# A planned order for the projection of an attention layer, with half of the values moved behind the queries

## The chip, the core and the metric

The kernel runs on one core of one Trainium2 chip. Its time is the device time of one execution in microseconds; a kernel is given by the median of its runs. The engines are TensorE (PE; PEld is its load of the stationary operand), VectorE (DVE), ScalarE (ACT), GpSimd (POOL) and SyncE (SP), which issues the DMA transfers. Each engine works through its own instructions in order and waits on semaphores for the others. TensorE writes to PSUM, which here is cut into eight banks of 128 x 512 float32 values.

## The reference

A two-layer encoder works on 1024 tokens of width 1024. Only the first mixer, grouped-query attention, is touched by the change:

```
h   = rmsnorm(x, attn_norm)
qkv = h @ w_qkv                   # 16 query heads, 4 key heads, 4 value heads of 64
q   = rope(rmsnorm(q, q_gain)) * 64 ** -0.5
k   = rope(rmsnorm(k, k_gain))    # row and column rotation over a grid of width 64
p   = softmax(q @ k.T)            # 1024 x 1024 for each query head
x   = x + concat(p @ v) @ w_o
```

Behind it come, in both layers, a cross attention into 256 memory tokens and a gated MLP with a convolution, and in the second layer a pooling mixer. All of that stays as it is.

## The kernel before, in words

**Numbers in two parts.** A float32 product is made of three TensorE products on a rounded high part and a low remainder (`mm3`, L738 to L743: high x high, high x low, low x high). A split is a copy on ScalarE (L668) and a subtraction on VectorE (L669).

**Tiles of the projection.** `attention` (L757) works on eight tiles of 128 tokens. The row tile is loaded (`load`), its root mean square is taken on ScalarE and GpSimd (`row_rstd`, L719), the row is scaled on VectorE (L727), turned on TensorE (L735) and split into the slots `hT`. A piece of the weights is 1024 x 256, loaded in two halves of 512 KB into row buffers `scr` (six in all) and split into a pair of slots (`stage_piece`, L679). There are a piece for the keys, one for the values and one for each of four groups of query heads, which is staged twice, once for each half of the tokens. One product of a tile with a piece has 24 TensorE instructions (`piece_gemm`).

**Heads.** Each key or query tile of 128 x 256 then goes through a chain: square on ScalarE (L835), sum on VectorE (L836), root on GpSimd (`rstd`, L714 and L716), scaling (L842), two crossed multiplies (L849) and a straight one (L851) with the tables on VectorE, an add on GpSimd (L852), a split on ScalarE and VectorE (keys L857 and L858, queries L668 and L669 on `qst`), a turn on TensorE (keys L865, queries L878), and copies out of PSUM (L868, L879). The tables of cosine and sine are made on GpSimd from `rope` and the two gains (`tables`, L798 to L819).

**The order of the steps.** The loop `step(i)` (L942) runs over 40 items: eight items of a key and a value tile, then 32 query tiles (half, group, tile). Step i splits item i - 3 and rotates item i - 2, stages a quarter of the next weight piece, prepares row i + 2, does the products of item i and turns item i - 4. The lag is thus fixed, and each engine gets its instructions in the order in which the steps name them. Behind the last three items the scores of the first three units are added (`early`, L788, called at L960).

**Behind the projection.** `units` are 128 pairs of a query block and a head. `scores` (L766) makes a 128 x 1024 score in the bank pair pA (L776), its maximum (L780), the exponential with its sum (L783), the inverse (L785) and the scaling on GpSimd (L786). `turn_p` turns and splits the probabilities, `values` (L996) multiplies them with the values (L1007, L1008). During the projection there is one pA and six banks pB, during the attention two and four.

**The planner.** Class `Plan` (L157) is used by the later stages of the kernel. An operation is added with a kind (engine, least time, time per element, delay, L163), keys that it reads and writes, and places in pools that it takes. `run` gives TensorE's operations their order as they were added; a due time for each of the others follows backwards from those that need them, and a list scheduler with these estimated costs then issues the operations of all engines, at most 30 us ahead of their due time.

Of the kernel before, what the change touches and what calls it, by code (L numbers as in the profile page):

```python
# [40 lines left out]
TA, E0, ES, EN = 0, 3, 2, 3  # L41
# [583 lines left out]
class Kernel:  # L625
# [131 lines left out]
    def attention(self):  # L757
# [8 lines left out]
        def scores(u):  # L766
            if u in prs:
                return
# [5 lines left out]
            for kh in range(2):  # L774
                for part in range(2):
                    nc.tensor.matmul(s[:, kh * 512:(kh + 1) * 512], q,  # L776
                                     R.v(K[part][kh], 4)[:, kv],
                                     start=part == 0, stop=part == 1)
            nm = self.stat(1, "nm")
# [8 lines left out]
        def early(u):  # L788
            if u < EN:
                scores(u)  # L790

        with tc.tile_pool(name="qk", bufs=1, reuse_waits="tile") as qk, self.psum("psq", 1, 6) as self.ps:
            T = [qk.tile([P, 2048], F32R, name=f"T{i}") for i in range(2)]
            wk, wv, w0 = [T[0], T[1]], [R.get(), R.get()], [R.get(), R.get()]
            gain = None
            tabs = {}

            def tables():  # L798

                tab = qk.tile([P, NT, 2, HD], F32, name="tab")  # L800
                nc.sync.dma_start(out=tab.rearrange("p t i c -> p t (i c)"),
                                  in_=a["rope"].rearrange("(t p) c -> p t c", p=P))
                gq = self.cst.tile([P, HD], F32, name="gq")
                gk = self.cst.tile([P, HD], F32, name="gk")
                for g, row in ((gq, a["attn_q_gain"][0]), (gk, a["attn_k_gain"][0])):
                    nc.sync.dma_start(out=g, in_=bass.AP(tensor=row.tensor, offset=row.offset, ap=[[0, P], [1, HD]]))
                nc.gpsimd.tensor_scalar(gq, gq, HD ** -0.5, 1.0, op0=OP.mult, op1=OP.mult)
                tk = self.scr().rearrange("p (t i c) -> p t i c", t=NT, i=2)
                for dst, g in ((tk, gk), (tab, gq)):
                    nc.gpsimd.tensor_tensor(out=dst[:, :, 0], in0=tab[:, :, 0],  # L810
                                            in1=g[:, None, :].to_broadcast([P, NT, HD]), op=OP.mult)
                    d6, t6 = (x[:, :, 1].rearrange("p t (x i c) -> p t x i c", x=2, i=2) for x in (dst, tab))
                    g4 = g.rearrange("p (x i c) -> p x i c", x=2, i=2)
                    for x in range(2):
                        for i in range(2):
                            nc.gpsimd.tensor_tensor(out=d6[:, :, x, i], in0=t6[:, :, x, i],
                                                    in1=g4[:, None, x, 1 - i].to_broadcast([P, NT, ROPE_PAIRS]),
                                                    op=OP.mult)
                tabs["k"], tabs["q"] = tk, tab  # L819

            hT = [[R.get() for _ in range(4)] for _ in range(2)]

            def lhs(t):
                return lambda k: self.blk(hT[t // 4], k, slice((t % 4) * P, (t % 4 + 1) * P))

            def piece_gemm(p, t, ws):
                wh, wl = (self.R_(s).rearrange("p (a b) -> p a b", a=8) for s in ws)
                for k in range(NK):
                    ah, al = lhs(t)(k)
                    self.mm3(p, ah, al, wh[:, k], wl[:, k], k == 0, k == NK - 1)  # L830

            def head_rstd(p):
                ss = self.stat(4, "ss4")
                sq = qk.tile([P, 256], F32, name="sq", bufs=2)
                nc.scalar.activation(sq, p, AF.Square)  # L835
                nc.vector.tensor_reduce(ss, sq.rearrange("p (h c) -> p h c", h=4), axis=AX.X, op=OP.add)  # L836
                return self.rstd(ss, 4, HD)

            def roped(p, r, tab, t):
                qn = qk.tile([P, 256], F32, name="qn", bufs=2)  # L840
                q3 = qn.rearrange("p (h c) -> p h c", h=4)
                nc.vector.tensor_tensor(out=q3, in0=p.rearrange("p (h c) -> p h c", h=4),  # L842
                                        in1=r[:, :, None].to_broadcast([P, 4, HD]), op=OP.mult)
                b = qk.tile([P, 256], F32, name="rb", bufs=2)
                q5 = qn.rearrange("p (h x i c) -> p h x i c", h=4, x=2, i=2)
                b5 = b.rearrange("p (h x i c) -> p h x i c", h=4, x=2, i=2)
                s5 = tab[:, t, 1].rearrange("p (x i c) -> p x i c", x=2, i=2)
# [13 lines left out]
            def turn_k(kst, t):  # L861
                for i in range(2):
                    p = self.psB().rearrange("p (a b) -> p a b", a=4)
                    for h in range(4):
                        nc.tensor.transpose(p[:, h, :], kst[:, h, i:i + 2].rearrange("p a b -> p (a b)").bitcast(F32),  # L865
                                            self.ident)
# [1033 lines left out]
```

## Time and profile before

| what | us |
| --- | --- |
| median of 3 runs | 2549.89 |
| lowest and highest run | 2549.88 and 2550.58 |
| the profiled execution, its own time | 2550.72 |
| its span in the profile | 2548.9 |
| TensorE busy | 2497.3 (98%) |
| VectorE busy | 1992.3 (78%) |
| ScalarE busy | 1344.8 (53%) |
| GpSimd busy | 386.7 (15%) |

The span runs from the first to the last instruction in the trace; the time of the execution has some overhead around it. A row of a timeline gives start, duration, engine, line and operation with its tiles; a bracket at its end gives the idle time of the engine before it and what ended it. A row of the table of stretches gives busy time and number of instructions for each engine, then the granted TensorE clock, the share of time that the DMA engines were busy, and the GB/s that they moved. A row of the waits gives the waiting instruction, what it waited for, the sum in us, how often, and the longest. A row of the groups gives how often an instruction came, its busy time, the mean duration in ns and the idle time before it. TensorE counts as busy while any matmul is in flight, and a matmul's duration overlaps that of the next, so the pace is read from start to start.

### The profile page before, as it was taken

The numbers are of one execution on the slowest core, as the hardware profiler recorded it, in microseconds if no ns is written. First come the engines' busy times: TensorE is split into PE (matmuls) and PEld (weight loads), VectorE is DVE, ScalarE is ACT, GpSimd is POOL, SyncE is SP. The second block draws the span as 40 slices with busy tenths as digits, with TensorE's granted clock in tenths as the row PEclk, the third lists the DMA queues.
The fourth block names the chain that finished last, engine by engine and source line by source line (L and its number), as shares of the span: only waits on it lengthen the run. The fifth ranks groups of instructions, "written<-read, shape, count | busy, mean of one in ns | idle before, by whom it ended". The sixth has DMA issues, their size and how long they took to land.

```text
span 2548.9 us, 37005 instructions
## 1 busy us (share of the span) xinstructions
PE 2497.3 (98%) x13481; PEld 2135.8 (84%) x13481; DVE 1992.3 (78%) x2937; ACT 1344.8 (53%) x2286; POOL 386.7 (15%) x533
## 2 busy tenths in 40 slices
PE   7999999999999999999999999999999999999998
PEld 7998888888889888888887888889888888887886
DVE  5778999993886479888878776887559888887775
ACT  4547888872545346554455433655436545545441
POOL 3564555540002000000000002102000000000001
PEclk9999999999999999999999999999999999999999
DMA  4200000032486123433447663388223324337651
GB/s 151 83 18 1 1 1 1 1 122 86 141 299 230 64 67 111 124 103 88 120 149 257 209 195 104 115 281 282 78 74 108 112 85 122 104 110 265 232 186 66
DMA packets 296203, 315.20 MB, mean 124 GB/s; under 512 B 12501, under 2 KB 235069, under 8 KB 296021
## 3 DMA queue, kind: packets, MB, share of 16 engines
q1 hardware_dynamic: 296021, 312.84, 37.6%
q8 instruction: 106, 1.74, 0.3%
q14 instruction: 76, 0.62, 0.1%
HBM read 227.23 MB, written 80.74 MB: 121 GB/s over the span
## 4 chain that ended last, share of the span: by engine, by line
PE 80%; DVE 9%; issue 3%; ACT 3%; POOL 2%; DMA 2%; SPq 0%; DVEq 0%; ACTq 0%; POOLq 0%
PE pB L741 21%; PE pB L743 21%; PE pB L742 21%; PE pA L743 3%; PE pA L741 3%; PE pA L742 3%; DVE nm L780 2%; PE pB L735 2%; PE pA L776 2%; PE pB L1007 1%; POOL qn L852 1%; DVE R L663 1%; DVE PT L669 1%; PE pB L1008 1%; ACT scr L783 1%
## 5 line engine op out<-in xcount | busy, mean ns | idle before, releaser
L741 PE MATMUL pB<-R,R 128*128 128x512 f32 (+1 forms) x2750 | 1023.4, 372 | 7.9 <-DVE scr L435 1.6
L742 PE MATMUL pB<-R,R 128*128 128x512 f32 (+1 forms) x2750 | 1016.2, 370 | 0.2 <-DVE R L669 0.2
L743 PE MATMUL pB<-R,R 128*128 128x512 f32 (+1 forms) x2730 | 1008.8, 370 | 3.6 <-DVE R L663 3.5
L741 PEld LDWEIGHTS pB<-R,R 128*128 128x128 f32 x2750 | 518.1, 188 | 102.2 <-DVE R L663 3.4
L743 PEld LDWEIGHTS pB<-R,R 128*128 128x128 f32 x2730 | 514.3, 188 | 92.1 <-DVE R L663 5.3
L742 PEld LDWEIGHTS pB<-R,R 128*128 128x128 f32 x2750 | 518.3, 188 | 86.4 <-DVE R L669 0.7
L660 ACT ACTIVATE R<-scr 128x512 fp32r<-128x512 f32 (+2 forms) x318 | 237.0, 780 | 238.8 <-DMA scr<-Gs 59.6
L663 DVE TENSOR_TENSOR R<-X,R 128x512 fp32r<-128x512 f32 x374 | 252.1, 685 | 65.7 <-ACT R L660 64.9
L660 ACT ACTIVATE R<-X 128x512 fp32r<-128x512 f32 x374 | 231.7, 630 | 133.8 <-PE pB L742 65.5
L663 DVE TENSOR_TENSOR R<-scr,R 128x512 fp32r<-128x512 f32 (+2 forms) x318 | 271.0, 882 | 23.8 <-ACT R L660 23.8
L714 POOL TENSOR_SCALAR ms<-ss 128x1 f32<-128x1 f32 (+2 forms) x102 | 24.4, 239 | 1715.3 <-ACT R L722 661.5
L433 ACT COPY scr<-pB 128x512 f32<-128x512 f32 x156 | 91.2, 586 | 196.9 <-PE pB L743 191.0
L786 POOL TENSOR_SCALAR scr<-scr,inv 128x1024 f32<-128x1024 f32 x128 | 144.5, 1129 | 165.8 <-DVE inv L785 160.9
L783 ACT ACTIVATE scr<-pA,nm 128x1024 f32<-128x1024 f32 x128 | 143.1, 1118 | 44.5 <-DVE nm L780 41.9
L669 DVE TENSOR_TENSOR PT<-pB,PT 128x512 fp32r<-128x512 f32 x256 | 163.7, 680 | 2.8 <-ACT PT L668 1.8
L1570 DVE TENSOR_TENSOR X<-pB,X 128x512 f32<-128x512 f32 x144 | 99.2, 690 | 78.9 <-PE pB L743 76.3
L780 DVE TENSOR_REDUCE nm<-pA 128x1 f32<-128x1024 f32 x128 | 156.0, 1219 | 0.5 <-PE pB L735 0.3
L735 PE MATMUL pB<-ident,scr 128*128 128x128 f32 x1088 | 144.6, 276 | 9.1 <-DVE scr L727 7.9
L741 PE MATMUL pA<-R,R 128*128 128x512 f32 (+1 forms) x416 | 149.5, 359 | 2.5 <-ACT R L660 2.5
L735 PEld LDWEIGHTS pB<-ident,scr 128*128 128x128 f32 x1088 | 124.2, 142 | 32.7 <-POOL scr L786 14.9
L743 PE MATMUL pA<-R,R 128*128 128x512 f32 (+1 forms) x416 | 148.9, 358 | 0.5 <-DVE R L663 0.5
L742 PE MATMUL pA<-R,R 128*128 128x512 f32 (+1 forms) x416 | 148.6, 357 | 0.5 <-DVE R L663 0.5
(145 smaller groups left out, 3535.9 us busy)
## 6 DMA issues: line engine op xcount, KB each, us to landing
X<-in_ffn_w_up SPq DMA_DIRECT2D x82, 512.0 KB
Gs<-X SPq DMA_DIRECT2D x100, 256.0 KB
scr<-in_ffn_w_down SPq DMA_DIRECT2D x44, 512.0 KB
scr<-Gs SPq DMA_DIRECT2D x56, 384.0 KB
scr<-Wt SPq DMA_DIRECT2D x40, 512.0 KB
scr<-in_xattn_w_kv SPq DMA_DIRECT2D x32, 512.0 KB
scr<-Gs SPq DMA_DIRECT2D x28, 512.0 KB
scr<-in_attn_w_qkv SPq DMA_DIRECT2D x20, 512.0 KB
```

What stands on the lines that cost most here:

```text
L433: self.nc.scalar.copy(out, p)
L660: self.nc.scalar.activation(hi, src, AF.Copy)
L663: self.nc.vector.tensor_tensor(out=lo, in0=src, in1=hi.bitcast(F32), op=OP.subtract)
L669: nc.vector.tensor_tensor(out=lo, in0=src, in1=hi.bitcast(F32), op=OP.subtract)
L735: self.nc.tensor.transpose(p[:, k, :], src[:, b * P:(b + 1) * P], self.ident)
L741: mm(out, ah, bh, start=start, stop=False)
L742: mm(out, ah, bl, start=False, stop=False)
L743: mm(out, al, bh, start=False, stop=stop)
L780: nc.vector.tensor_reduce(nm, s, axis=AX.X, op=OP.max, negate=True)
L783: nc.scalar.activation(pr, s, AF.Exp, bias=nm, accum_out=rs)
L786: nc.gpsimd.tensor_scalar(pr, pr, ri, 1.0, op0=OP.mult, op1=OP.mult)
L1570: nc.vector.tensor_tensor(out=x, in0=banks[b], in1=x, op=OP.add)
```

## The change

The loop of steps and its helpers are replaced by a plan. What is computed for each tile is the same; the order of the instructions on every engine is now found by `Plan.run`. TensorE's own order is given by a new list, and the turn of an item stands `LAG` = 4 products behind its product:

```diff
-TA, E0, ES, EN = 0, 3, 2, 3
+QKV = (("K", 0), ("V", 0), ("K", 1), ("V", 1), ("K", 2), ("V", 2), ("K", 3), ("V", 3),
+       ("K", 4), (0, 0, 0), (0, 0, 1), ("K", 5), (0, 0, 2), (0, 0, 3), ("K", 6), (0, 1, 0), (0, 1, 1), ("K", 7), (0, 1, 2), (0, 1, 3),
+       *((h, g, t) for h in range(2) for g in range(4) if h or g > 1 for t in range(4 * h, 4 * h + 4)),
+       ("V", 4), ("S", 0), ("V", 5), ("S", 1), ("V", 6), ("S", 2), ("V", 7))
+LAG = 4
```

Keys and values alternate only for the first four tiles. Keys 4 to 7 stand between the first eight queries (half, group, tile), and the values of tiles 4 to 7 stand behind all queries, each followed by one of the three early scores. Since the value weights have been overwritten by then, they are staged a second time (`late`):

```diff
+                    if kind == "V":
+                        if t == 0:
+                            plan_weights("V", (NH + NKV) * HD, 1)
+                        elif t == 4:
+                            plan_weights("late", (NH + NKV) * HD, 0)
```

Every operation becomes an entry with its kind, its size and its keys. The head of a key or query tile:

```diff
+                plan.add("copy", 350, square, [b], [sq], [("sq", sq)], [b])
+                plan.add("add", 340, reduce, [sq], [ss], uses=[sq])
+                plan.add("scale", 2.9, rstd, [ss], [ss])
+                plan.add("add", 340, scaled, [b, ss], [qn], [("qn", qn)], [b])
+                plan.add("add", 490, crossed, [qn, tabkey], [rb], [("rb", rb)], [qn, *used])
+                plan.add("add", 360, straight, [qn, tabkey], [qn], uses=[qn, *used])
+                plan.add("scale", 2.4, both, [qn, rb], [qn], uses=[qn, rb])
```

A product with its places, the split of a value tile, and the early scores:

```diff
+                plan.add("product", 12.4, emit, [("hT", t, g) for g in range(2)] + [("w", s, g) for g in range(2)], [b],
+                         [("B", b)], gives=gives)
...
+                plan.add("copy", 360, lambda: self.high(v[:, :, :HD], src()), [b], [("V", t)], uses=[b])
+                plan.add("add", 340, lambda: self.low(v[:, :, :HD], v[:, :, HD:], src()), [b, ("V", t)], [("V", t)], uses=[b])
...
+                plan.add("tap", 1024, biggest, [s], [("nm", u)], uses=[s])
+                plan.add("square", 1024, exp, [s, ("nm", u)], [x], [("scr", None)], [s], late=4.0)
+                plan.add("tiny", 1, inverse, [x], [("inv", u)], late=6.0)
+                plan.add("scale", 2.7, scale, [("inv", u), x], [x], late=7.0)
```

The tables are no longer made in one go: load, scaling, cosine and sine of both tables are entries of their own (`plan_tables`), as are load, square, norm, turn and split of a row (`plan_rows`) and load and split of each weight half (`plan_weights`). The pools are declared as six `scr`, one pA, six pB, two each of `sq`, `qn` and `rb`, three `qst` and the free slots.

Two things follow for the instruction streams. TensorE's number of instructions stays the same. VectorE and ScalarE get two instructions more and SP two loads more, for the second staging of the value weights. From the fourth score on (the start of the attention) all five engines have the same instructions in the same order as before.

More of the change, by code (lines that the diff above doesn't have):

```diff
@@ new lines, in plan_turn_k, with turn, put @@
+            def plan_turn_k(t):
+                half = ("kst", t)
+                for i in range(2):
+                    b = ("kturned", t, i)
+                    def turn(i=i, b=b):
+                        kst = R.hv(at[half])[:, :768].rearrange("p (h i c) -> p h i c", h=4, i=3)
+                        p = at[b] = self.psB().rearrange("p (a b) -> p a b", a=4)
+                        for h in range(4):
+                            nc.tensor.transpose(p[:, h, :], kst[:, h, i:i + 2].rearrange("p a b -> p (a b)").bitcast(F32),
+                                                self.ident)
+                    def put(i=i, b=b):
+                        o = R.v(K[i][t // 4], 4)[:, :, (t % 4) * P:(t % 4 + 1) * P]
+                        (nc.vector.tensor_copy if i else nc.scalar.copy)(o, at.pop(b))
+                    plan.add("turn", 4, turn, [half], [b], [("B", b)], [half])
+                    plan.add("add" if i else "copy", 512, put, [b], [("KT", t, i)], uses=[b])
```

398 lines of the change are left out of this document (228 added, 170 removed).

## The prediction

> **What bounds the kernel now.** I read the stretches of 20 us first, then TensorE's waits before 206 us (the first weighted sum of values starts at 206.38), then the timeline of each engine where these pointed. Behind that point the two kernels issue the same instructions in the same order on all five queues; only buffer and DMA queue numbers differ. So the whole difference is made in the first 206 us, and all that follows moves with it.
>
> ```profile
> core 0: us, PE busy (x) PEld busy (x) DVE busy (x) ACT busy (x) POOL busy (x), PEclk, DMA share, GB/s
> 20.00:40.00 20.00, 17.24 (x124) 17.04 (x123) 8.42 (x16) 6.22 (x13) 10.50 (x19) 0.83 0.25 85
> 180.00:200.00 20.00, 13.76 (x81) 11.02 (x80) 14.59 (x34) 8.94 (x20) 11.50 (x16) 0.74 0.00 1
> ```
> ```profile
> PE pB L735 <- DVE scr L727: 7.9, 1, 7.9
> PE pB L878 <- DVE qst L669: 6.5, 6, 2.6
> PE pB L743 <- DVE R L669: 3.9, 3, 2.8
> ```
>
> TensorE is the bound, with three holes: the start (7.9 us until the first row is normalised), the stretch from 20 to 40 us, and the one around 180 to 200 us. In the last two the granted clock falls as well, to 0.83 and 0.74.
>
> The pace between the holes is that of the query tiles: 24 products and a turn of four transposes.
>
> ```profile
> 120.76 0.60 PE L878 MATMUL pB<-ident,qst 128*128 128x128 f32 x4
> 121.11 0.36 PE L741 MATMUL pB<-T,R 128*128 128x256 f32 x1
> 124.00 0.60 PE L878 MATMUL pB<-ident,qst 128*128 128x128 f32 x4
> ```
>
> A turn takes 0.35 us from start to start, the 24 products 2.89, together 3.24; four queries need 12.96.
>
> The chain of the head (square, sum, root, scale, rotate, add, split) is slower. In the chain of waits GpSimd's add comes back at
>
> ```profile
> 112.14 1.60 POOL qn L852
> 126.30 1.59 POOL qn L852
> ```
>
> that is every 14.16 us for four queries (the two other long ones between belong to the same four). So from query to query TensorE uses up its lag of four steps; by the end the chain is late:
>
> ```profile
> 186.04 1.09 PE L776 MATMUL pA<-R,R 128*128 128x512 f32 x4
> 187.29 0.63 PE L878 MATMUL pB<-ident,qst 128*128 128x128 f32 x4 [0.15 <-DVE qst L669]
> 190.23 1.12 PE L878 MATMUL pB<-ident,qst 128*128 128x128 f32 x4 [2.31 <-DVE qst L669]
> 193.97 1.09 PE L878 MATMUL pB<-ident,qst 128*128 128x128 f32 x4 [2.63 <-DVE qst L669]
> 199.32 1.11 PE L878 MATMUL pB<-ident,qst 128*128 128x128 f32 x4 [0.38 <-DVE qst L669]
> 203.79 1.03 PE L735 MATMUL pB<-ident,scr 128*128 128x128 f32 x8
> 204.58 1.17 PE L776 MATMUL pA<-R,R 128*128 128x512 f32 x4
> 206.38 0.36 PE L1007 MATMUL pB<-PT,R 128*128 128x256 f32 x1
> ```
>
> The last product ends at 186.04 (the second score starts there); the last query is turned 13.28 us later, and between them TensorE has nothing but turns and scores.
>
> **The change, part by part.**
>
> *The tail.* From 186.04 to 206.38 are 20.34 us. At full pace this holds five query turns (0.35 each), scores 1 and 2 (0.94 each, bounded from 187.29 - 186.04 = 1.25 with its wait and taken from the 0.9 to 1.0 that a score takes at 204.58), and then three turns of probabilities (203.79 to 204.58: 0.79) with scores 3 and 4 between them: 1.75 + 1.88 + 2.37 + 1.88 = 7.9. The hole is 12.4 us. The change takes four products of values, 4 x 2.89 = 11.6 us, out of the front and lays them here, with the three scores between them. TensorE's order is now: turn, V4, turn, S0, V5, turn, S1, V6, turn, S2, V7, turn, then the attention. Counted from the end of the last query's product, at full pace: V4 ends at 3.2, S0 at 4.5, V5 at 7.4, S1 at 8.7, V6 at 11.6, S2 at 12.9, V7 at 15.8, the last turn at 16.1, and with the 4.25 of probabilities and scores values could start at 20.4.
>
> What is late next? There is one score buffer (pA), so S1 waits for the exponential of S0:
>
> ```profile
> L780 DVE TENSOR_REDUCE nm<-pA 128x1 f32<-128x1024 f32 x4 | 4.9, 1214 | 0.0
> L783 ACT ACTIVATE scr<-pA,nm 128x1024 f32<-128x1024 f32 x4 | 4.5, 1119 | 3.0 <-DVE nm L780 3.0
> L668 ACT ACTIVATE R<-pB 128x512 fp32r<-128x512 f32 (+1 forms) x24 | 11.8, 525 | 25.5 <-PE pB L743 19.3 <-PE pB L735 6.2
> L879 ACT CAST R<-pB 128x512 fp32r<-128x512 f32 x32 | 18.6, 580 | 0.2 <-PE pB L878 0.2
> ```
>
> S0 ends at 4.5, its maximum (1.21) at 5.8, its exponential (1.12 and the read of the sum) at 7.1: before 7.8, when S1 is due. VectorE stands at the maximum of S0 from about 1 to 4.5 with the split of query 37 behind it; that split is done at 6.1 and its turn due at 7.4. The next two splits, behind the maximum of S1, end by 10.4 and 12.2 and are due at 11.6 and 15.8. So no turn waits. But in ScalarE's order the copies of V5, V6 and V7 and of the last three queries stand behind the exponential of S2, which ends at 15.5: three at about 0.4 (half rows; bounded by 0.52, the mean of the mixed group) and three at 0.58, some 2.7 us, to 18.2. The split of the first probabilities is behind them. From there copy, subtraction, maximum and the second subtraction bring the first values to 22.3 instead of 20.4. On equal work the kernel before needs 20.34 + 11.6 + 0.94 (S0 was issued earlier) = 32.9; the new one 22.3. **Gain 10.6.** Bounds: 12.5 if the copies cost nothing, 8 if the six banks make the last turns wait for them once more (2.7).
>
> *The front.*
>
> ```profile
> 17.81 1.28 DVE L727 SCALAR_TENSOR_TENSOR scr<-scr,rs 128x1024 f32<-128x1024 f32 x1 [0.72 <-POOL rs L716]
> 23.11 1.03 PE L735 MATMUL pB<-ident,scr 128*128 128x128 f32 x8
> 26.84 0.28 PE L741 MATMUL pB<-T,R 128*128 128x256 f32 x1
> 30.00 0.58 PE L743 MATMUL pB<-T,R 128*128 128x256 f32 x1 [2.76 <-DVE R L669]
> 34.87 0.41 PE L735 MATMUL pB<-ident,scr 128*128 128x128 f32 x1
> 28.06 1.28 DVE L727 SCALAR_TENSOR_TENSOR scr<-scr,rs 128x1024 f32<-128x1024 f32 x1 [5.88 <-POOL rs L716]
> 29.27 1.61 DVE L669 TENSOR_TENSOR R<-pB,R 128x512 fp32r<-128x512 f32 x3
> 24.01 1.74 POOL L816 TENSOR_TENSOR tab<-tab,gq 128x128 f32<-128x128 f32 x4
> ```
>
> The third key tile's products take 34.87 - 26.84 = 8.03 us instead of 2.89. The low half of its rows (29.27) stands on VectorE behind the norm of the next row (28.06), and this behind eleven table instructions in one run on GpSimd, the last at 24.01, and a head's root. The plan sets the roots between the table instructions, and the low half ahead of the next norm. Followed through: GpSimd now takes the first key table before the root of row 2, so that norm moves from 17.8 to about 21.7, just before its turn at 23.1; the key tables end near 25.5, the low half near 27.5, and the products wait 0.6 instead of 2.76, with less of the slow clock (0.58 for a 0.28 product). **Gain 4.5**, between 0 (the root stays late) and 5.1.
>
> *Smaller waits* of TensorE come from the old order of steps too:
>
> ```profile
> 46.65 0.38 PE L743 MATMUL pB<-T,R 128*128 128x256 f32 x1 [0.51 <-DVE R L669]
> 62.67 0.38 PE L741 MATMUL pB<-T,R 128*128 128x256 f32 x1 [0.98 <-DVE R L669]
> ```
>
> These are 1.5, and once the lag is used up each four queries take 14.16 instead of 12.96; for the last two groups before 186 us that is 2.4 more (an estimate from the two paces). Of 3.9 I take **3**, between 0 and 4.5 (with restarts).
>
> *The middle.* Keys 4 to 7 now run beside eight queries. VectorE's rows:
>
> ```profile
> L836 DVE TENSOR_REDUCE ss<-sq 128x4 f32<-128x256 f32 x40 | 16.6, 414 | 4.3 <-ACT sq L835 4.3
> L842 DVE TENSOR_TENSOR qn<-pB,rs 128x256 f32<-128x256 f32 x40 | 16.7, 417 | 0.4 <-POOL rs L716 0.4
> L849 DVE TENSOR_TENSOR rb<-qn,tab 128x128 f32<-128x128 f32 x64 | 15.8, 287 | 1.0
> L669 DVE TENSOR_TENSOR T<-scr,T 128x1024 fp32r<-128x1024 f32 x10 | 12.2, 1220 | 1.5 <-ACT T L668 1.5
> ```
>
> A head costs 0.41 + 0.42 + 2 x 0.29, and about 0.42 each for its second multiply and its split: 2.25, twelve heads 27; two norms 2.6, six low halves of rows 3.9, six key copies 4.1, five or six weight halves 6 to 7. That is 44 us, some 41 when overlapping issue is taken off, against TensorE's 43 (twelve products, three row turns, five key and five query turns). Level, but with a lag of four products ahead of each turn I cost it at nothing; if the cover is gone it costs up to 4.
>
> *Added:* the value weights are fetched and split a second time: two loads of 512 KB on SP (the DMA is idle there), two copies on ScalarE, two subtractions of 1.22 on VectorE. Each lies in the query stretch, where TensorE needs 12.96 per four queries. I put four queries of the new VectorE order in line by hand (head steps of neighbouring queries interleaved instead of one after the other): 12.2 with both weight halves. So the chain no longer loses time on TensorE: 0, at worst 14.16 - 12.96 = 1.2 for each of the six last groups, 7.
>
> [...]
>
> ```profile
> 165.64 0.74 POOL L852 TENSOR_TENSOR qn<-qn,rb 128x256 f32<-128x256 f32 x1 [1.00 <-DVE qn L851]
> 195.51 0.73 POOL L852 TENSOR_TENSOR qn<-qn,rb 128x256 f32<-128x256 f32 x1 [1.23 <-ACT R L879]
> 195.56 0.95 DVE L851 TENSOR_TENSOR qn<-qn,tab 128x256 f32<-128x256 f32 x1
> ```
>
> GpSimd's add takes 0.74 by itself and 1.6 beside a weight subtraction; VectorE's multiply takes 0.95 instead of 0.42 when the add started first. The new order puts rotations of the next query beside this add. My 12.2 already lets each rotation wait for the add. [...]
>
> **The sum.** 10.6 + 4.5 + 3 = 18.1 us. The profiled execution took 2550.72 (span 2548.9), the median is 2549.89; the difference of 0.8 is small against the terms, and I take the sum off the median: **2532**.
>
> **The rivals.**
> [...]
> 2. *The plan doesn't do what it says*: its costs are estimates, and a turn placed behind a late copy opens new waits, so that the tail's 10.6 is given back. For: the one score buffer, and six banks all held at the last turn. Against: the due times above. Gain about 0 to 5: 2547.
> 3. *Slower*: a weight half that lands late. The loads share the row buffers: four are free beside gain and key table. ScalarE's copy of a half stands ahead of the squares, so a load that must wait for the turn of the next row (a row comes every 11 us: key, two queries and turns) stops all heads for up to 11 us, 8 of them beyond one query step. Three such halves cost 24 against the gain of 18, +6: 2556. It decides when more than two of the eight halves in the middle wait so. Against: in the order in which buffers come free, SP waits for the turn of the row before, not of the next.
>
> **Chances.** Forecast 0.62 (2527 to 2537), rival 1 0.21, rival 2 0.09, rival 3 0.08. The bounds of the terms (12.5 + 5.1 + 4.5 = 22, and 8 + 0 + 0) give 2528 and 2542; range 2526 to 2543. A measurement can tell 0.2%, 5 us, from no change: faster 0.87, same 0.06, slower 0.07.
>
> **What would show it.** Right: no wait on `qst` over 0.5 us before the attention; TensorE busy and granted 1.00 in the 20 us before the first values, which start near 188; the third key tile's products under 4 us. [...]

## The result, and the profile after

The changed kernel takes 2533.73 us (median of 4 runs, 2531.66 to 2536.19) against 2550.23 us for the kernel before on the same chips: a ratio of 0.993, 95% interval 0.9913 to 0.9948. Timed again later it took 2533.46 us (5 runs) against 2550.47, ratio 0.9933 (0.9921 to 0.9945). That is 16.5 to 17 us less; 2532 was forecast. The profiled execution took 2532.28 us with a span of 2530.5.

The stretches of the changed kernel, to be set beside those of the prediction (columns: length, busy time and count of TensorE, its weight loads, VectorE, ScalarE and GpSimd, granted clock, DMA share, GB/s):

```profile
20.00:40.00 20.00, 18.26 (x154) 17.86 (x153) 14.26 (x26) 10.71 (x23) 16.64 (x27) 1.00 0.24 80
40.00:60.00 20.00, 20.00 (x174) 20.00 (x173) 17.52 (x35) 11.94 (x23) 11.64 (x16) 1.00 0.34 107
160.00:180.00 20.00, 20.00 (x163) 19.58 (x162) 16.11 (x38) 8.27 (x18) 13.13 (x16) 1.00 0.00 1
180.00:200.00 20.00, 18.86 (x139) 17.22 (x139) 16.38 (x27) 15.78 (x31) 6.90 (x7) 1.00 0.00 1
```

Where TensorE had 17.24 at a clock of 0.83 and 13.76 at 0.74, it now has 18.26 and 18.86 at 1.00, and from 40 to 180 us each stretch is full. All that TensorE waited for before 190 us (engine, tile and line, releaser: us in total, times, longest):

```profile
PE pB L856 <- DVE scr L851: 7.9, 1, 7.9
PE pB L747 <- DVE R L667: 1.7, 2, 1.1
PE pB L745 <- ACT R L664: 1.2, 1, 1.2
PE pB L739 <- ACT R L1020: 1.1, 1, 1.1
PE pB L988 <- DVE R L973: 0.7, 1, 0.7
```

The waits for a query's split (`qst`, 6.5 us before) are gone. What is left is the start (7.9) and single waits of 0.6 to 1.2 us. The tail, in TensorE's timeline (start, duration, line, tiles; in brackets the idle time before and its releaser):

```profile
167.36 0.60 PE L1014 MATMUL pB<-ident,qst 128*128 128x128 f32 x4
170.96 1.17 PE L778 MATMUL pA<-R,R 128*128 128x512 f32 x4
175.13 1.17 PE L778 MATMUL pA<-R,R 128*128 128x512 f32 x4
179.30 1.17 PE L778 MATMUL pA<-R,R 128*128 128x512 f32 x4
183.11 0.60 PE L1014 MATMUL pB<-ident,qst 128*128 128x128 f32 x4
185.29 0.66 PE L739 MATMUL pB<-ident,scr 128*128 128x128 f32 x4 [1.14 <-ACT R L1020]
189.29 0.37 PE L1133 MATMUL pB<-PT,R 128*128 128x256 f32 x1
```

The last query's products end at 167.36, the three scores lie 4.17 us apart with a product of values between each two, the last query is turned at 183.11, and the first weighted sum of values ("first values" from here on) starts at 189.29 instead of 206.38. So 17.1 of the 18.4 us between the spans are made before this point.

The third key tile:

```profile
28.17 0.28 PE L745 MATMUL pB<-T,R 128*128 128x256 f32 x1
29.65 0.39 PE L747 MATMUL pB<-T,R 128*128 128x256 f32 x1 [1.08 <-DVE R L667]
32.33 0.93 PE L856 MATMUL pB<-ident,scr 128*128 128x128 f32 x7
```

Its products take 32.33 - 28.17 = 4.16 us, against 8.03. That is just over the 4 us that the prediction named as a sign.

### The profile page after: what moved, and what is told of

It reads as the page before. It is cut to its first block, busy times and chain, and to the rows that moved or that the text cites. A ratio compares the mean times of both kernels' runs of the same rounds, so it can differ in the third digit from the quotient of the medians.

```text
span 2530.5 us, 37018 instructions
## 1 busy us (share of the span) xinstructions
PE 2488.5 (98%) x13481; PEld 2132.1 (84%) x13481; DVE 2000.4 (79%) x2939; ACT 1347.1 (53%) x2288; POOL 397.5 (16%) x533
## 4 chain that ended last, share of the span: by engine, by line
PE 85%; DVE 7%; issue 2%; ACT 2%; DMA 2%; POOL 1%; DVEq 0%; SPq 0%; ACTq 0%; POOLq 0%
PE pB L745 22%; PE pB L747 22%; PE pB L746 22%; PE pA L747 3%; PE pA L745 3%; PE pA L746 3%; PE pA L778 2%; DVE nm L788 2%; PE pB L739 2%; PE pB L1133 1%; DVE R L667 1%; DVE PT L673 1%; PE pB L1134 1%; ACT scr L791 1%; PE pB L323 1%
## 5 line engine op out<-in xcount | busy, mean ns | idle before, releaser
L664 ACT ACTIVATE R<-scr 128x512 fp32r<-128x512 f32 (+2 forms) x330 | 250.2, 791 | 240.6 <-PE pB L746 56.2
L718 POOL TENSOR_SCALAR ms<-ss 128x1 f32<-128x1 f32 (+2 forms) x102 | 34.3, 336 | 1694.5 <-ACT R L726 661.3
L667 DVE TENSOR_TENSOR R<-scr,R 128x512 fp32r<-128x512 f32 (+2 forms) x330 | 285.1, 893 | 18.8 <-ACT R L664 18.3
L778 PE MATMUL pA<-R,R 128*128 128x512 f32 x512 | 145.1, 405 | 0.0
L672 ACT ACTIVATE PT<-pB 128x512 fp32r<-128x512 f32 x256 | 138.8, 596 | 11.1 <-PE pB L739 10.2
```

Source lines behind the costliest of these rows:

```text
L664: self.nc.scalar.activation(hi, src, AF.Copy)
L667: self.nc.vector.tensor_tensor(out=lo, in0=src, in1=hi.bitcast(F32), op=OP.subtract)
L672: nc.scalar.activation(hi, src, AF.Copy)
L778: nc.tensor.matmul(s[:, kh * 512:(kh + 1) * 512], q, R.v(K[part][kh], 4)[:, kv], start=part == 0, stop=part == 1)
```

## The experiments

The prediction's largest term says that the tail is empty and the moved values fill it. The rival reading, formed after the first result, is that the tail is long because the heads come late, and that their order alone would shorten it. As everything before the attention shows in the time of the first values, I give that time for each run beside the whole. "Behind" is the profiled span less the first values. Both come from one profiled execution for each run; the changed kernel's two profiles have their first values 0.6 us apart, so steps of that size in this column say little.

Each ratio is to the kernel before on the same chip, where it took 2551.31 us (experiments 1 to 4), 2550.47 (the changed kernel again, 5 to 7), 2551.54 (8 to 10) and 2550.63 (11). The changed kernel was run a second time beside some of the others:

> The changed kernel once more, unchanged, so that the others of this call can be set against it: 2532 to 2536, first values at 188 to 190 us.

| kernel | median us (runs) | ratio to before on the same chip, 95% | first values | behind |
|---|---|---|---|---|
| before | 2550.23 (4) | 1 | 206.38 | 2342.5 |
| changed | 2533.73 (4) | 0.993 (0.9913 to 0.9948) | 189.29 | 2341.2 |
| changed, again | 2533.46 (5) | 0.9933 (0.9921 to 0.9945) | 188.71 | 2344.8 |
| 1 values in front | 2548.67 (11) | 0.999 (0.9981 to 0.9999) | 200.78 | 2347.2 |
| 2 before, stages exchanged | 2544.0 (6) | 0.997 (0.9959 to 0.9982) | 197.06 | 2345.7 |
| 3 before, values behind | 2549.78 (11) | 0.9994 (0.9985 to 1.0003) | 200.63 | 2346.8 |
| 4 before, query tables later | 2548.37 (11) | 0.9988 (0.9979 to 0.9997) | 202.24 | 2343.2 |
| 5 before, all three | 2540.22 (5) | 0.9958 (0.9945 to 0.997) | 192.43 | 2345.3 |
| 6 tables in one run | 2537.74 (5) | 0.9946 (0.9934 to 0.9959) | 190.50 | 2345.4 |
| 7 staged twice | 2538.25 (5) | 0.9952 (0.9939 to 0.9966) | 190.69 | 2345.4 |
| 8 scores last | 2546.51 (11) | 0.9981 (0.9972 to 0.999) | 202.18 | 2343.9 |
| 9 copies early | 2536.61 (5) | 0.9945 (0.9933 to 0.9958) | 190.36 | 2343.3 |
| 10 scores early | 2534.31 (5) | 0.9934 (0.992 to 0.9947) | 188.35 | 2345.6 |
| 11 three more | 2535.67 (5) | 0.994 (0.9926 to 0.9954) | 189.43 | 2343.3 |

### 1. The plan without the moved values

```diff
-       ("K", 4), (0, 0, 0), (0, 0, 1), ("K", 5), (0, 0, 2), (0, 0, 3), ("K", 6), (0, 1, 0), (0, 1, 1), ("K", 7), (0, 1, 2), (0, 1, 3),
-       *((h, g, t) for h in range(2) for g in range(4) if h or g > 1 for t in range(4 * h, 4 * h + 4)),
-       ("V", 4), ("S", 0), ("V", 5), ("S", 1), ("V", 6), ("S", 2), ("V", 7))
+       ("K", 4), ("V", 4), ("K", 5), ("V", 5), ("K", 6), ("V", 6), ("K", 7), ("V", 7),
+       *((h, g, t) for h in range(2) for g in range(4) for t in range(4 * h, 4 * h + 4)))
...
-                        elif t == 4:
-                            plan_weights("late", (NH + NKV) * HD, 0)
...
-                for _, f in todo:
+                for n, (_, f) in enumerate(todo):
                     if f:
                         f()
+                    if n < 3:
+                        plan_scores(n)
```

> The changed kernel with the values of tiles 4 to 7 back among the keys; nothing is staged twice, and the three early scores stand between the last turns. The plan stays. Theory F (what the prediction's largest term says: behind the last query TensorE has a hole of 12.4 us, and only moved products fill it): it loses about 10.6 us against the changed kernel, 2543 to 2545, with some 20 us from the end of the last product to the first values. Theory C (the hole is mostly the late chain of the heads, and the plan brings the chain on time whatever the tail holds): last turn some 7 us behind the last product instead of 13.3, scores then 3.5 us apart for the one score buffer, first values 12 to 14 us behind the last product; it loses only 2 to 5 us, 2535 to 2539.

TensorE's timeline of this kernel, from the end of the last query's product (178.70):

```profile
178.70 0.60 PE L1013 MATMUL pB<-ident,qst 128*128 128x128 f32 x4
180.52 0.66 PE L1013 MATMUL pB<-ident,qst 128*128 128x128 f32 x4 [1.22 <-DVE qst L666]
180.93 1.17 PE L777 MATMUL pA<-R,R 128*128 128x512 f32 x4
184.18 0.63 PE L1013 MATMUL pB<-ident,qst 128*128 128x128 f32 x4 [2.07 <-DVE qst L666]
188.48 0.73 PE L777 MATMUL pA<-R,R 128*128 128x512 f32 x2 [1.78 <-ACT scr L1042]
192.32 1.09 PE L738 MATMUL pB<-ident,scr 128*128 128x128 f32 x8 [2.21 <-ACT scr L1042]
200.78 0.37 PE L1132 MATMUL pB<-PT,R 128*128 128x256 f32 x1
```

The tail takes 22.1 us: turns wait for splits, the third score and the first turn of probabilities wait for exponentials. First values come 11.5 us later than in the changed kernel. Theory F said 10.6, theory C at most 5. With the plan, then, it is the moved values that shorten the tail. (Its tail without them is also 6.3 us longer than that of the next experiment, which holds one score less.) The whole time is 4 to 6 us above what F gave; most of that lies behind the first values and is taken up at the end.

### 2. The old steps with two stages exchanged

```diff
-                for lag, stage in ((3, split), (2, rope)):
+                for lag, stage in ((2, rope), (3, split)):
```

> The kernel before, with the two stages of a step exchanged: a head is rotated before the split of the head before it, so VectorE's low half no longer waits for GpSimd's add and ScalarE's copy ahead of the next rotation. Nothing else. Theory F: the chain's pace falls from 14.16 to about 12.2 us per four queries, TensorE's waits for the query's split of 2.4 us go, and the tail keeps its hole: gain 2 to 3, 2547 to 2548. Theory C: the turns of the tail come on time too (2.31 and 2.63 and most of the 13.28 us to the last turn): gain 7 to 10, 2540 to 2543. If the order of the two stages is not what sets the chain's pace: 2550.

TensorE's timeline:

```profile
181.31 1.09 PE L776 MATMUL pA<-R,R 128*128 128x512 f32 x4
186.88 1.92 PE L776 MATMUL pA<-R,R 128*128 128x512 f32 x4 [2.44 <-ACT scr L783]
190.45 1.11 PE L878 MATMUL pB<-ident,qst 128*128 128x128 f32 x4 [0.79 <-DVE qst L669]
197.06 0.37 PE L1007 MATMUL pB<-PT,R 128*128 128x256 f32 x1
```

What VectorE waited for in the kernel before, from 60 to 180 us, in the first row of that view:

```profile
DVE qst L669 <- ACT qst L668: 21.4, 26, 1.0
```

One exchanged pair brings the first values forward by 9.3 us, and here theory C is right: the last product ends at 181.31 instead of 186.04 (4.7 us), and the tail behind it takes 15.75 us instead of 20.34 (4.6). In the old order VectorE's low half of a head stood ahead of the next rotation and waited for GpSimd's add and ScalarE's copy, 21.4 us in all; behind the rotation it waits for neither, and this row is gone from the same view. The hole of 12.4 us thus had two causes: late heads (4.6) and, as the next experiment and the fifth show, too little work beside the scores (the rest). The whole time, 2544.0, is 1 us above theory C's range.

### 3. The old steps with the values behind

```diff
-                if i < NT:
-                    piece_gemm(p[:, :256], i, wk)
-                    turn_h(i + 1)
-                    piece_gemm(p[:, 256:], i, wv)
+                if i < NT or i >= len(items):
+                    if i < NT:
+                        piece_gemm(p[:, :256], i, wk)
+                        turn_h(i + 1)
+                        if i >= 4:
+                            rs[i] = head_rstd(p[:, :256])
+                            return
+                        piece_gemm(p[:, 256:], i, wv)
+                    else:
+                        ps.pop(i)
+                        i -= len(items) - 4
+                        piece_gemm(p[:, 256:], i, wv)
...
+                if n == len(order):
+                    return self.stage_piece(w, (NH + NKV) * HD, wv)
...
-                if 0 <= i < len(items):
+                if 0 <= i < len(items) + 4:
```

> The kernel before, steps and lag as they were, with the values of tiles 4 to 7 computed in the four steps behind the last query and their weights staged a second time. Theory F: the hole is filled without any plan: gain 8 to 11, 2539 to 2542. Theory C: the four products cover the late chain, so the gain is of the same size here, 7 to 10, but it is not to be had a second time beside the exchanged stages. Rival (the fixed steps can't use it: copies of the values and the late splits stand in each other's way, or keys 4 to 7 without a second product run into VectorE): gain under 4, over 2546.

TensorE's timeline, beside the fifth key tile and at the end:

```profile
49.19 0.38 PE L741 MATMUL pB<-T,R 128*128 128x256 f32 x1 [0.62 <-ACT R L868]
51.29 0.39 PE L743 MATMUL pB<-T,R 128*128 128x256 f32 x1 [1.60 <-DVE R L669]
200.63 0.37 PE L1021 MATMUL pB<-PT,R 128*128 128x256 f32 x1
```

The last query's product ends at 177.3 (the fourth of the last group in the timeline). From there to the first values are 23.3 us; with the first score, which is issued ahead here, 24.3 on the work of the prediction's 32.9: 8.6 gained in the tail, within the 8 to 11 of theory F. But 5.75 is all that arrives. Keys 4 to 7 now follow each other with one product of 2.9 us each, and these wait for the low halves of the rows and for ScalarE's copies; TensorE is busy 16.24 of the 20 us from 40 to 60, where it had 19.49, and the granted clock there is 0.91 instead of 1.00. That is 3.3 us and about 1.8 (0.09 x 20): some 5 us. And 2.4 us of the 5.75 are not the edit's, which changes nothing before the fifth key tile: the third waits only 1.46 us in this execution, the clock stays at 1.00 behind it, and the turn of the fourth row starts at 32.48 instead of 34.87. The ratio's interval contains 1: alone this edit can't be told from no change.

### 4. The old steps with the query's tables later

```diff
                 if i == 0:
                     tables()
+                if i == 4:
+                    tabs["rest"]()
```

Here `tables` ends with the key's half.

> The kernel before, with the query's half of the table instructions on GpSimd moved from the first step to the fifth; the key's half stays. Prediction's reason (the root of the fourth row and of the first head stand behind eleven table instructions): the third key tile's products take 3 to 4.5 us instead of 8.03, gain 3.5 to 4.5, 2545 to 2547. Rival (the row's low half is late for another reason, VectorE's order): products stay at 7 to 8 us, 2550.

```profile
26.76 0.28 PE L741 MATMUL pB<-T,R 128*128 128x256 f32 x1
29.90 0.27 PE L735 MATMUL pB<-ident,scr 128*128 128x128 f32 x1
```

In TensorE's timeline the third key tile's products take 29.90 - 26.76 = 3.14 us, and first values come 4.1 us earlier. The long run of table instructions ahead of the roots was the cause in the kernel before. The median is 2.9 us below that of the kernel before on this chip, less than the 3.5 to 4.5 expected.

### 5. All three, without a plan

> The kernel before with its steps and lag, and the three edits together: the query's tables in the fifth step, a head rotated before the split of the head before it, and the values of tiles 4 to 7 behind the queries. No plan. Alone they brought the first values forward by 4.1, 9.3 and 5.75 us. Theory A (three separate terms that add up): 19.2 us, first values at 187, 2529 to 2533. Theory B (the exchange and the moved values both work on the same hole of 12.4 us in the tail, 4.6 and 8.6 of it, and the moved values leave keys 4 to 7 without cover): 4.7 + 4.1 - 2.9 and 9 to 11 for the tail, 15 to 17 us, first values at 189.5 to 191.5, 2533 to 2537. Theory C (only the plan's order on VectorE makes the gain): over 2540.

First values at 192.43: 13.95 us of the changed kernel's 17.1, and 5.2 less than the three gains added. By the medians it is less, 10.3 of 17.0. Theory A is out, theory B is missed by 0.9 us, and C is out in its strong form, though the whole time is at C's bound. The first row below is the stretch that the plan still does better; the second is the second score, which starts where the last query's product ends:

```profile
40.00:60.00 20.00, 16.38 (x121) 15.30 (x120) 17.10 (x32) 10.47 (x20) 12.39 (x18) 0.91 0.36 117
```
```profile
172.45 1.09 PE L776 MATMUL pA<-R,R 128*128 128x512 f32 x4
```

TensorE has 16.38 at a clock of 0.91 where the changed kernel has 20.00 at 1.00: 3.6 us and about 1.8 by the clock. There the changed kernel lays two queries between each two keys, which the old steps have not; that order in the old steps was not tried. Only 3.1 us lie between the first values, because the old steps are ahead elsewhere: from 20 to 40 us TensorE has 19.95 against 18.26, and the tail takes 192.43 - 172.45 = 19.98 us, with the first score, which is issued ahead, 20.9 against the plan's 21.93.

So in the tail the two edits nearly add up: 4.6 and 8.6 alone, 32.9 - 20.9 = 12.0 of the hole's 12.4 together. What doesn't add up lies mostly in front. The turn of the fourth row, right behind the third key tile, starts at 34.87 in the kernel before, at 34.12, 32.48 and 29.90 in experiments 2, 3 and 4, and at 29.93 here: 0.75 and 2.4 us of the hole that experiment 4 closes had been counted in experiments 2 and 3 as well.

### 6. The tables in one run, within the plan

```diff
-                for z, n in (("K", 2.9), ("Q", 2.9)):
...
+                def both():
+                    scaled()
+                    for z in "KQ":
+                        cos(z)
+                        for x in range(2):
+                            sin(z, x)
+                plan.add("scale", 14.7, both, ["tab", "gK", "gQ"], [("tab", "K"), ("tab", "Q"), "tab", "gQ"], [("scr", "tabK")])
```

> The changed kernel with the eleven table instructions of GpSimd in one run again, as one step of the plan; the root of the third row then stands behind them. If the front's gain comes from the roots standing between the table instructions: the third row's norm ends near 32 instead of 23, TensorE waits 7 to 8 us for its turn, first values near 197, 2540 to 2542. If the front's gain has another cause: within 2 us of the changed kernel.

```profile
27.38 1.06 PE L856 MATMUL pB<-ident,scr 128*128 128x128 f32 x8 [2.67 <-DVE scr L851]
```

A miss: this wait in TensorE's timeline is 2.67 us, not 7 to 8, and as the third key tile then finds its rows ready, first values are only 1.2 us later. I had reckoned with a longer run; it took 6.0 us (19.10 to 25.0 on GpSimd), about what it took in the kernel before (6.2, 19.52 to 25.75). By the expectation's own bound (within 2 us) the place of the roots is thus not the main part of the front's gain within the plan: the turn of the fourth row starts 1.7 us later (33.99 against 32.33), still before the 34.87 of the kernel before. That the low half now stands ahead of the next norm, the other half of the prediction's reason, was not tried alone.

### 7. The late weights staged twice

```diff
                             plan_weights("late", (NH + NKV) * HD, 0)
+                            plan_weights("late2", (NH + NKV) * HD, 0)
```

> The changed kernel with the late value weights staged twice, one after the other into the same place: two more loads, two more copies on ScalarE and two more subtractions of 1.22 us on VectorE in the query stretch. Forecast's reason (this work lies beside TensorE's): first values later by 0 to 0.5 us, 2533 to 2535. Rival (VectorE has no room left: its 2.4 us come out on TensorE, or the loads stop ScalarE): 2.4 to 7 us later, 2536 to 2541.

```profile
168.63 0.63 PE L1014 MATMUL pB<-ident,qst 128*128 128x128 f32 x4 [1.86 <-DVE qst L667]
```

First values come 1.4 us later than at 189.29, with one new wait of 1.86 us in TensorE's timeline: between the two expectations. The median, 2538.25, lies in the rival's range, but most of its excess arises behind the first values. Counted from the first key's turn (L988, at 33.12 here and 34.02 in the changed kernel) the loss is 2.3 us, nearly all of the 2.4 added on VectorE. The first staging is hidden, the next no longer is. The cover ends here.

### 8. The scores behind the values

```diff
-       ("V", 4), ("S", 0), ("V", 5), ("S", 1), ("V", 6), ("S", 2), ("V", 7))
+       ("V", 4), ("V", 5), ("V", 6), ("V", 7), ("S", 0), ("S", 1), ("S", 2))
```

> The changed kernel with the four products of values in a row and the three early scores behind them, instead of between. If the tail is filled only because the score buffer's chain (score, maximum, exponential, 3.3 to 3.5 us for each) runs beside the values: scores start at about 180.4 and follow one another every 3.5 us, first values at 193 to 194, 4 to 5 us later, 2537 to 2539. If the four products alone do it: first values within 1 us, 2533 to 2535.

What TensorE waited for from 180 to 202 us, and the stretch:

```profile
PE pA L778 <- ACT scr L1043: 5.1, 2, 2.6
PE pB L739 <- ACT scr L1043: 2.6, 1, 2.6
PE pB L739 <- ACT R L1020: 1.1, 1, 1.1
```
```profile
180.00:200.00 20.00, 11.15 (x39) 7.94 (x39) 8.05 (x12) 7.59 (x15) 3.36 (x3) 0.60 0.00 0
```

12.9 us later, not 4 to 5. The direction was right: the second and third score wait for the exponential ahead of them, as there is one score buffer. What I left out is the clock, 0.60 in this stretch, and that the first turn of probabilities waits for the last exponential. Four moved products with the scores behind them give 202.18, later than the 200.78 of experiment 1, which moves nothing. The gain of the tail hangs on other work standing beside the chain of the scores; experiment 10 shows that products of queries do as well as the values.

### 9 and 10. What is left of the tail

```diff
-                plan.add("copy", 360, lambda: self.high(v[:, :, :HD], src()), [b], [("V", t)], uses=[b])
+                plan.add("copy", 360, lambda: self.high(v[:, :, :HD], src()), [b], [("V", t)], uses=[b], late=1.0)
...
-                    plan.add("copy", 512, put, [bank], [("QT", g, half, t)], uses=[bank], room=(("Q", g, half), 2))
+                    plan.add("copy", 512, put, [bank], [("QT", g, half, t)], uses=[bank], room=(("Q", g, half), 2), late=2.0)
```

The low half of the values gets `late=2.0` as well.

> The changed kernel with due times given to the copies of the values (late 1 and 2) and of the turned queries (late 2), so that in ScalarE's order they stand ahead of the exponentials of the tail, not behind the last one; nothing else. If the 1.1 us that the first turn of probabilities waits, and what follows it, come from these late copies (the prediction's 1.9 us): no such wait, first values 1 to 2 us earlier, 187.3 to 188.3, 2532 to 2533. If the exponentials themselves set the end of the tail, they now come later by the copies: first values 0 to 2 us later, 2534 to 2536.

TensorE's timeline:

```profile
185.71 1.30 PE L739 MATMUL pB<-ident,scr 128*128 128x128 f32 x8 [0.43 <-ACT scr L1043]
```

The wait for the late copy (1.14) is gone, and one of 0.43 for the exponential stands in its place. From the last query's product (168.93 here) to first values are 21.43 us instead of 21.93: 0.5 us. The first values are later all the same, because the third key tile waited longer (2.63). Of the prediction's 1.9 us for late copies only 0.5 can be had by putting the copies first; then the exponential is what the turn waits for.

```diff
-       ("V", 4), ("S", 0), ("V", 5), ("S", 1), ("V", 6), ("S", 2), ("V", 7))
+       ("S", 0), (1, 3, 5), ("S", 1), (1, 3, 6), ("S", 2), (1, 3, 7), ("V", 4), ("V", 5), ("V", 6), ("V", 7))
```

> The changed kernel with the three early scores between the last queries' products instead of between the values. If the rest of the tail's hole (1.5 us) is the scores' chain with the copies behind it: TensorE has no wait left before the first values, which come 1 to 1.5 us earlier, 187.8 to 188.3, 2532 to 2533. Rival: three maxima of 1.2 us and three exponentials of 1.1 us in the query stretch make the splits of the queries late: waits on the query's split, first values 1 to 3 us later, 2534.5 to 2537.

First values at 188.35, 0.94 earlier than in the first profile of the changed kernel and 0.36 earlier than in the second, with one wait of 0.4 left in the tail; 2534.31 us, which is not less than the changed kernel. The tail is as good as full either way. The values stand in a row here too, as in experiment 8, but the chain of each score runs beside a product of queries or values, and nothing is lost.

### 11. Three more edits on the changed kernel

```diff
+            p = self.psB()
+            for _ in range(24):
+                nc.tensor.transpose(p[:, :P], self.ident, self.ident)
...
+                    hold = ["hold"] if z == "Q" else []
+                    plan.known["hold"] = 38.0
```

(and experiment 10's order; `hold` is read by the query's table entries)

> The changed kernel with three edits that the runs so far suggest: the three early scores between the last queries' products; the query's table instructions held back to about 38 us, out of the third key tile's way; and 24 transposes of the identity, whose results nobody reads, on TensorE from about 1.3 us, while it waits for the first row, so that the clock is granted in full when the first key tile comes (its products now start 0.213 us apart in place of 0.119). If the slow start is the clock's: 1 to 2.5 us from the first key tile, 0.5 to 1 from the third, 0.2 to 0.9 from the tail; first values at 185 to 187.3, 2529 to 2532. Rival (the splits of the first rows and weights on ScalarE and VectorE take up what TensorE wins, each product then waits for them): first values at 187.5 to 189, 2532 to 2534.

TensorE's timeline:

```profile
1.34 4.94 PE L803 MATMUL pB<-ident 128*128 128x128 f32 x24 [1.34 <-POOL ident masks.py:199]
7.99 1.09 PE L861 MATMUL pB<-ident,scr 128*128 128x128 f32 x8 [1.70 <-DVE scr L856]
11.16 0.38 PE L745 MATMUL pB<-T,R 128*128 128x256 f32 x1 [2.08 <-ACT R L664]
12.53 0.58 PE L747 MATMUL pB<-T,R 128*128 128x256 f32 x1 [0.88 <-DVE R L667]
15.90 0.30 PE L747 MATMUL pB<-T,R 128*128 128x256 f32 x1
```

A miss: 2535.67 us and first values at 189.43 are later than even the rival said. The transposes did speed up TensorE: the first row's turn takes 1.09 instead of 1.97. But its products can't start before 11.16, when ScalarE has split the rows, and over the holes of 1.70, 2.08 and 0.88 us that is lost again: the granted clock is 0.50 in each 1 us stretch from 13 to 15, and from 12.53 to 15.90 most products take 0.41, behind that 0.28. In the second profile of the changed kernel the slow products end at 15.8 without any transposes. No run beat the changed kernel.

## Why the prediction was right

- **Sum.** 18.1 us were forecast; 17.1 show at the first values and 16.5 to 17 in the medians. The sum is nearer than its terms: the front gave less, the smaller waits more, and the slow start of this execution took 1.3 (see the front).
- **Tail, 10.6.** Measured 32.9 - 21.9 = 11.0, and 11.5 from the other side (experiment 1). The mechanism holds, with three things that the working passed over. Of the 12.4 us, 4.6 could also be had by exchanging two stages; over the exchanged steps, whose tail on equal work is 15.75 + 11.6 + 0.9 = 28.3, the moved values are worth 7.4 (experiment 5). And the interleaved scores are no detail: with nothing beside their chain the gain is gone (experiment 8), so the one score buffer, which stood among the arguments for rival 2, does decide. That kernel's 2546.51 is rival 2's 2547. The late copies were put at 1.9 and cost 0.5. The third is the clock. The old tail, and the part of it in which the granted clock is 0.50:

```profile
186.04:206.38 20.34, 13.77 (x63) 10.14 (x61) 15.14 (x32) 10.74 (x22) 8.66 (x11) 0.66 0.00 0
189.60:203.20 13.60, 8.87 (x30) 6.39 (x31) 9.67 (x22) 7.39 (x16) 6.91 (x8) 0.50 0.00 1
```

  TensorE is idle for 6.6 of the 20.34 us. Of the 8.87 us in which it is busy at half clock, about half would be saved at full clock: 4.4 us (an estimate from the granted 0.50). So some third of the hole is the clock, which fell over the first wait of 2.31 us (187.92 to 190.23): it reads 1.00 from 188 to 189, 0.80 from 189 to 190 and 0.50 from 190 on. In the changed kernel, where the waits are filled, it is 1.00 from 180 to 200. Whether a full clock alone, without moved values, would win its part was not tried.
- **Front, 4.5.** The step that was mis-sized. The third key tile gains 8.03 - 4.16 = 3.87, and a new wait of 0.7 for the first key's turn (L988) takes some of it back: 3.2 are left. In the second profile the tile takes 4.71, and 2.7 are left. Besides, the tile starts 1.3 us later in the first profile (28.17 instead of 26.84). That is not the order's doing: the slow start, with products of 0.41 instead of 0.28 (the granted clock reads 1.00 there from 13 to 18 us), lasts beyond 17.2 us there, to 15.8 in the second profile and to 15.4 in the kernel before, and its end varies like this over the profiles of all the kernels. That the run of table instructions made the hole in the kernel before is shown in experiment 4; which part of the plan's order closes it is not (experiment 6). The missing part is in these rows of VectorE and GpSimd:

```profile
27.19 1.48 DVE L945 TENSOR_TENSOR qn<-qn,scr 128x256 f32<-128x256 f32 x1
28.92 1.27 DVE L667 TENSOR_TENSOR R<-pB,R 128x512 fp32r<-128x512 f32 x2
```
```profile
27.09 1.29 POOL L820 TENSOR_TENSOR tab<-tab,gq 128x512 f32<-128x512 f32 x1
```

  I had the low half end near 27.5; it starts at 28.92. The key tables end at 26.8 instead of 25.5, as two roots stand between them. And ahead of the low half VectorE's multiply takes 1.48 instead of 0.42, beside a table instruction of 1.29 on GpSimd that started 0.10 us before it. The prediction measured the same beside an add that had started first (0.95 instead of 0.42) and reckoned with it in the query stretch, not here.
- **Smaller waits, 3.** On equal work the last query's product ends 186.04 - 11.6 - 0.9 - 167.36 = 6.2 us earlier. Of this the front has 3.2, and the slow start took 1.3; so some 4.3 belong here, by subtraction.
- **Middle and second staging, 0.** Right: TensorE is full from 40 to 180 us. Experiments 3 and 5 give the price of the cover, some 5 us with the clock where no queries stand between the keys, and experiment 7 shows that the room behind the second staging is under 2.4 us of VectorE.
- **Chain.** GpSimd's adds in the changed kernel:

```profile
116.06 0.75 POOL L949 TENSOR_TENSOR qn<-qn,rb 128x256 f32<-128x256 f32 x1 [0.93 <-DVE qn L945]
154.99 0.74 POOL L949 TENSOR_TENSOR qn<-qn,rb 128x256 f32<-128x256 f32 x1 [0.93 <-DVE qn L945]
```

  Between them are twelve queries: 12.98 us for four, TensorE's own pace (12.96), and the add takes its undisturbed 0.74. Rival 1, in which the chain stays at its old pace of 14.16, did not come, and TensorE waits for no split. That an exchange of two stages is nearly enough for this (experiment 2: adds at 101.86 and 154.32, sixteen queries, 13.1 for four) was not seen.
- **Rival 3** did not come: after 40 us ScalarE waits for no load of `in_attn_w_qkv`.
- **"All that follows moves with it"** was too simple, as the next section but one shows.

## What to carry to other kernels

A hole at the end of a stage is read twice: what is there to do (work that can be moved) and what is late (a chain that can be reordered). Here the answers gave 8.6 and 4.6 us alone and 12.0 together, and the hole of 12.4 is all that there is. Gains read at a later point add up worse (19.2 by single edits, 13.95 together), because single runs can close part of another hole by the way; so each edit is read in its own stretch. Moved work helps only if the links of the chain that makes the hole have work beside them, whichever work that is, and the place it is taken from must have other cover.

## What the runs showed of the hardware

**Behind the first values the time is not fixed.** TensorE, VectorE, ScalarE and GpSimd have the same instructions there in nearly all these kernels, yet "behind" runs from 2341.2 to 2347.2, and two profiles of the same changed kernel differ by 3.6. Their TensorE rows part at about 1349 and at 1600 us, where the granted clock of the second one dips:

```profile
1340.00:1350.00 10.00, 8.20 (x31) 6.30 (x30) 8.59 (x12) 4.82 (x6) 0.00 (x0) 0.86 0.98 312
1590.00:1600.00 10.00, 9.61 (x67) 9.39 (x67) 5.92 (x9) 3.77 (x7) 2.04 (x4) 0.83 0.18 70
```

The first profile has no dip there. In stretches of 1 us the first dip reads 0.63, 0.50, 0.50 and 0.66 from 1347 to 1351, the second 0.51, 0.50, 0.50 and 0.79 from 1593 to 1597. What is missing to 1.00 adds up to 1.7 us in each, as much as about 3.4 us at half clock. Several low clocks came with holes in TensorE's work: holes of 1.70, 2.08 and 0.88 us close together (experiment 11, 0.50 from 13 to 15), single waits of 2.31 and 2.63 us between short products in the old tail (0.50 from 189.60 to 203.20), and one hole of 1.80 us ahead of the dip at 1347. Behind other holes there is none: 1.49 us, ended at 1346.43, in the first profile (granted clock 1.00 from 1340 to 1360), and 2.67 us, ended at 27.38, in experiment 6 (the products behind it take 0.28). Which holes cost the clock is thus not settled by these runs.

**Left open.** The medians of the changed kernel and of the one before are lower, against their first values, than those of most experiments, by some 1 to 5 us. Only part of it is dips: experiment 7 has none between 210 and 2500 us and is still 4.2 slower behind than the first profile of the changed kernel. What makes up the rest was not found.
